# Paged decode of a hybrid layer step: all score products of a half batch in one run, six key buffers, and a first up pair of seven block products

## The chip, the cores and the metric

The kernel runs on one core of one Trainium2 chip. The metric is the device time of one launch in microseconds (us), the median of several runs; the time before is 1226.16 us. The core's engines work side by side, each through its own queue in order: TensorE (PE in the profile; PEld its weight loads), VectorE (DVE), ScalarE (ACT), GpSimd (POOL) and SyncE (SP, which issues most of the weight transfers).

## The reference

One layer of a hybrid decoder for 512 prompt tokens and 8 x 4 sample tokens, all in float32:

```python
def layer(h, pos, past_ckv, past_kr, ...):
    h = h + 0.5 * rmsnorm(swiglu(rmsnorm(h, norm_g[0]), wg[0], wu[0], wd[0]), norm_g[1])
    m, c_kv, k_r, s_fin = mixer(rmsnorm(h, norm_g[2]), ...)      # HGRN2 heads and latent attention heads
    h = h + rmsnorm(m, norm_g[3])
    h = h + 0.5 * rmsnorm(swiglu(rmsnorm(h, norm_g[4]), wg[1], wu[1], wd[1]), norm_g[5])
    return h, c_kv, k_r, s_fin
```

In the mixer each sample token attends to 4096 cached positions, whose latents (256 wide) and rotary keys (64 wide) lie in pages that a page table scatters over a pool. A score is the product of query and latent plus the product of the rotary parts; then softmax, then the weighted sum of the latents:

```python
s = (einsum('bqhr,bsr->bhqs', q_lat, c_kv) + einsum('bqhd,bsd->bhqs', q_rope, k_rope)) * scale
p = softmax(where(k_pos <= q_pos, s, -inf))
o = einsum('bhqs,bsr->bqhr', p, c_kv)
```

## The kernel before

The kernel keeps the layer's activations on the chip and streams the weights. Matrix products are made of three products of a high and a low half of each operand: `split` (lines 157 to 159) casts a tile to its high part on ScalarE and subtracts for the low part on VectorE, so every weight tile and every activation passes both engines (`wh` and `wl`, `uh` and `ul`, and so on).

**The decode.** The paged attention of the samples runs in small steps between the products of the mixer's big gemms (line 248), from about 705 to 920 us. Its 8 sample sequences are 16 half batches (class `Half`). A half gathers two blocks of latents (`gather`, into the slots `ma`, `dx0`, `dx1`, `q0`, `ha`, `hb`, `mb`) and their rotary keys (`rraw`) by indirect transfers. `turn` (line 1498) transposes them on VectorE into key tiles `kh`, one of five stages at a time, two transposes each; there are `KHB` = 4 buffers for `kh`. `score` (line 1510) makes eight small products for a stage, 64 rows by 32 columns of TensorE's array, so 40 for a half. When the last stage is done, ScalarE copies the odd half of the scores and VectorE adds and takes the maximum (`top`, line 1519). `peak` (from line 1523) spreads the maximum by a product `pm`, VectorE reduces it and makes the softmax's bias, ScalarE exponentiates, VectorE transposes the result (`pt`), and six copies on ScalarE and two on VectorE place it in `pbuf`. `value` (line 1546) then makes 16 products of `pbuf` and the latents.

The generator `decode` sets the order: for a half in step n come its `turn` in the steps after it, its scores two steps later, its peak and values three steps later. `RUNS` says in which of the five steps which stages are scored:

```python
RUNS = {2: (0, 1, 2), 4: (3, 4)}
```

so three stages (24 products) run in the middle step and two (16) in the last. Where these pieces come to stand between the gemm's products is decided ahead of the launch, by the scheduler that orders each engine's instructions; the early halves are cut into smaller pieces by it.

**The second FFN.** Gate and up weights come as pairs j = 4 to 10 of 128-column tiles (`tile_pair`). A pair takes one of two forms. `classic` (the products at line 230) makes four sums, each of 24 products of 128x272. `seven` (the products at line 449) makes seven block products of 12 each, in the banks X, Y and Z, from sums of the weight blocks (`S` and the in-place sums, lines 480 to 486) and of the activation blocks (`T1` to `T3` and the blocks `B11`, `B12`, `B21`, `B22`); ScalarE copies a bank to `tq` and VectorE adds up the results (line 498). Before, the first gate pair and the first up pair (j = `J0` = 4) are classic. Between the two, VectorE makes the activation sums for the later pairs, and the last of them, `split(*B12, Z)`, overwrites `B12`, which the classic up pair still reads; so it stands at the start of j = 5.

Of the kernel before, what the change touches and what calls it, by code (L numbers as in the profile page):

```python
# [15 lines left out]
ALU = mybir.AluOpType  # L16
# [43 lines left out]
NW = 2  # L60
PRE, BODY = 22, 95
JS = ((8, 9), (0, 1), (2, 3), (4, 5), (6, 7))
KHB = 4
PEAK = 1
RUNS = {2: (0, 1, 2), 4: (3, 4)}
LEVELS = (32, 16, 8, 4, 2, 1)
CH = 64

# [39 lines left out]
def hybrid_step_kernel(  # L108
# [18 lines left out]
    def mk(shape, dt, tag, bufs=1, pool=None):  # L127
        return (pool or cur[-1]).tile(shape, dt, name=tag, tag=tag, bufs=bufs)
# [28 lines left out]
    def split(hi, lo, src, eng=None):  # L157
        nc.scalar.copy(hi, src)  # L158
        (eng or nc.vector).tensor_tensor(lo, src, f32(hi), op=ALU.subtract)  # L159
# [160 lines left out]
    def raw_pair(src, f):  # L320
        return [raw(src, f + i) for i in range(2)]
# [15 lines left out]
    def wsplit(w, step=KD):  # L337
        ws = ring()
        for k in range(0, KD, step):
            split(*parts(ws, slice(k, k + step)), w[:, k : k + step])  # L340
        return ws
# [1078 lines left out]
    with scope("dec"):  # L1420
# [48 lines left out]
        class Half:  # L1469
# [31 lines left out]
            def score(self, st):  # L1501
                q = qbd[self.b % 2]
                if st == 0:
                    self.s = [ps("s", own=True) for _ in range(2)]
                for jj, j in enumerate(JS[st]):
                    for g in range(2):
                        c = (2 * jj + g) * 32
                        for r in range(2):
                            rs = slice(r * 64, r * 64 + 64)
                            nc.tensor.matmul(self.s[r][c : c + 32, : 2 * P], q[rs, j], self.kh[st][rs, g, :, jj], start=st == 0, stop=st == len(JS) - 1, skip_group_check=True)  # L1510
                if st == 1 and self.i and self.b + 1 < NB:
                    qsplit(self.b + 1)
                if st < len(JS) - 1:
                    return
                odd = mk([64, 2, 2 * P], F32, "odd")
                self.mx = mk([P, 1], F32, "mxh", 2)
                for r in range(2):
                    nc.scalar.copy(odd[:, r], self.s[r][64:, : 2 * P])
                    self.top = nc.vector.tensor_tensor_reduce(self.e[r * 64 : r * 64 + 64], self.s[r][:64, : 2 * P], odd[:, r], 1.0, -3.0e38, ALU.add, ALU.max, self.mx[r * 64 : r * 64 + 64])

            def peak(self):
                pm = ps("pm", "pm")[:, :P]
                nc.tensor.matmul(pm, self.mx.broadcast_to([P, P]), ident, start=True, stop=True, skip_group_check=True)
                m = m3[:, self.i, self.bs]
                nc.vector.tensor_reduce(m, pm.rearrange("p (g q) -> p q g", q=16), axis=AX.X, op=ALU.max)
                mq = mk([P, 16], F32, "mq", 2)
                mb = mk([P, 1], F32, "mbd", 2)
                nc.vector.scalar_tensor_tensor(mq, m, -SCALE, selL, op0=ALU.mult, op1=ALU.mult, accum_out=mb)
                nc.scalar.activation(self.e, self.e, AF.Exp, scale=SCALE, bias=mb, accum_out=Lc[:, self.i, 0, self.b : self.b + 1])
                pt = mk([P, ROWS, 32], F32, "pt", 2)  # L1530
                nc.vector.transpose(pt.rearrange("p a k -> p (a k)"), self.e)
                for r in range(2):
                    for g in range(2):
                        for h_ in range(2):
                            src = pt[(2 * r + g) * 32 : (2 * r + g) * 32 + 32, :, h_ * 16 : h_ * 16 + 16]
                            to = self.p[(2 * r + h_) * 32 : (2 * r + h_) * 32 + 32, g, :, self.i * 16 : self.i * 16 + 16]
                            (nc.scalar.copy if g + h_ else nc.vector.tensor_copy)(to, src)
# [19 lines left out]
        def decode():  # L1557
# [19 lines left out]
            for n in range(NH2 + 4):  # L1577
# [3 lines left out]

                for st in range(len(JS)):
                    if at(2):
                        for k in RUNS.get(st, ()):
                            at(2).score(k)
                    if n < 2 and st == 0:
                        if n == 0:
# [152 lines left out]
    with scope("ffn1") as pool:  # L1740
# [14 lines left out]
            nc.vector.tensor_tensor(mT[x][:, d], mT[x][:, d], acc, op=ALU.add)  # L1755

        def tile_pair(j, src, C, mid=None):
            if j == J0:
                w = ws.pop() if ws else [wsplit(w) for w in raw_pair(src, 2 * j)]
                classic(w, C, 0, ucol)  # L1760
                with tc.issue_after(mark[2]):
                    next(sc, None)
                classic(w, C, 1, ucol)
                if mid:
                    mid()
            else:
                seven(raw_pair(src, 2 * j), C, mid, sc if j < 7 else iter(()))

# [7 lines left out]
        for j in range(J0, NF // 2):  # L1776
            if j > J0:
                late = G, V
            G, V = (c[:, j % 2] for c in Cq)
            if j == J0 + 1:  # L1780
                with tc.issue_after(mark[0]):
                    split(*B12, Z)
            if j == 7:
                mT = [actslot("m", x, n=W2) for x in BOTH]
                for x in BOTH:
# [9 lines left out]
            if j == J0:  # L1795
# [9 lines left out]
                nc.vector.tensor_tensor(Z, f32(B21[0]), f32(B21[1]), op=ALU.add)  # L1805
                split(*T2, Y)
                nc.vector.tensor_tensor(Z, Z, Y, op=ALU.subtract)
            else:
                H = [mk([P, 2, 2, W2], F32R, n, 3) for n in ("hh", "hl")]
                with tc.issue_after(mark[0]):  # L1810
# [140 lines left out]
```

## Time and profile before

| | |
|---|---|
| median of the runs | 1226.16 us (1226.01 to 1227.58) |
| the profiled run, its own time | 1225.88 us |
| its span | 1224.0 us (1.88 us lie outside) |
| TensorE busy | 1197.8 us, 98% |
| weight loads busy | 1092.4 us, 89% |
| VectorE busy | 986.6 us, 81% |
| ScalarE busy | 693.6 us, 57% |
| GpSimd busy | 97.7 us, 8% |

The numbers come from one execution recorded by the hardware profiler. Busy time of an engine is summed over its instructions; a row of the timeline has the start, the duration, the engine, the line of the kernel, the operation with output and inputs, and, in brackets, for how long the engine had been idle and what released it. Rows that follow one another on an engine and are alike stand as one, with their count behind an x.

### The profile page before, as it was taken

The page shows a single profiled execution, that of the slowest core. Times are in us where ns is not written, and L with a number is a line of the kernel's source. Part 1 is how long each engine was busy: PE and PEld are TensorE (multiplying, and loading weights), DVE is VectorE, ACT ScalarE, POOL GpSimd, SP SyncE. Part 2 cuts the span into 40 slices and gives each one's busy share as a digit, 9 for nine tenths or more (in the row PEclk, how much of TensorE's full clock was granted, in tenths as well). Part 3 has the DMA queues.
Part 4 walks back from the last instruction along what each step waited for, and adds up shares of the span by engine and source line. Part 5 has one row for each costly group of instructions (what it writes and reads, how often), then busy time and mean ns, then how long its engine had stood idle before and what let it go on. Part 6 is the DMA issues. An engine that isn't in the chain of part 4 may idle for free.

```text
span 1224.0 us, 26742 instructions
## 1 busy us (share of the span) xinstructions
PE 1197.8 (98%) x10924; PEld 1092.4 (89%) x10924; DVE 986.6 (81%) x2008; ACT 693.6 (57%) x1447; POOL 97.7 (8%) x112
## 2 busy tenths in 40 slices
PE   8999999999999999999999999999999999999997
PEld 7999999999999989998998876666667999999996
DVE  7997887878678788886877789888985789778665
ACT  7765554454476654554758765455444465554373
POOL 0000000000000000000000123332321111000000
PEclk9999999999999999999999999999999999999999
DMA  6233333323254313333242486679876858533451
GB/s 242 70 121 104 104 101 94 101 80 105 83 186 142 116 56 104 90 92 108 95 141 86 163 343 209 231 266 356 277 258 163 262 211 286 163 107 118 103 149 74
DMA packets 78427, 188.43 MB, mean 154 GB/s; under 512 B 14032, under 2 KB 35568, under 8 KB 73824
## 3 DMA queue, kind: packets, MB, share of 16 engines
q1 hardware_dynamic: 58128, 115.50, 28.8%
q0 software_dynamic: 15440, 65.67, 16.5%
q10 hardware_dynamic: 4736, 5.55, 1.3%
q8 instruction: 85, 1.39, 0.5%
q14 instruction: 38, 0.31, 0.1%
HBM read 170.53 MB, written 16.16 MB: 153 GB/s over the span
## 4 chain that ended last, share of the span: by engine, by line
PE 81%; issue 6%; DVE 5%; ACT 3%; DMA 3%; POOL 1%; DVEq 0%; SPq 0%; ACTq 0%; POOLq 0%
PE acc L248 18%; PE dn L230 12%; PE Y L449 11%; PE acc L230 8%; PE Z L449 7%; PE X L449 7%; PE acc L1853 3%; PE acc L628 3%; PE s L1510 3%; PE o L1546 2%; DVE kh L1498 1%; DMA ma<-w_g 1%; PE pa L976 1%; DMA mb<-w_u 1%; PE s L1226 1%
## 5 line engine op out<-in xcount | busy, mean ns | idle before, releaser
L248 PE MATMUL acc<-uh,wh 128*128 128x272 f32 (+2 forms) x496 | 160.9, 324 | 0.0
L248 PE MATMUL acc<-ul,wh 128*128 128x272 f32 (+2 forms) x496 | 156.3, 315 | 1.0 <-DVE ul L196 1.0
L248 PE MATMUL acc<-uh,wl 128*128 128x272 f32 (+2 forms) x496 | 155.7, 314 | 0.5 <-issue 0.5
L230 PE MATMUL dn<-hh,dh 128*128 128x272 f32 x384 | 111.3, 290 | 0.1
L230 PE MATMUL dn<-hh,dl 128*128 128x272 f32 x384 | 110.7, 288 | 0.0
L230 PE MATMUL dn<-hl,dh 128*128 128x272 f32 x384 | 110.5, 288 | 0.0
L222 DVE TENSOR_TENSOR wl<-wraw,wh 128x1024 fp32r<-128x1024 f32 (+2 forms) x78 | 83.6, 1074 | 31.7 <-ACT wh L221 31.1
L248 PEld LDWEIGHTS acc<-uh,wh 128*128 128x128 f32 x496 | 93.4, 188 | 17.1 <-issue 12.7
L221 ACT CAST wh<-wraw 128x1024 fp32r<-128x1024 f32 (+2 forms) x78 | 72.6, 932 | 57.8 <-PE acc L248 37.8
L248 PEld LDWEIGHTS acc<-ul,wh 128*128 128x128 f32 x496 | 93.5, 188 | 7.7 <-DVE ul L196 2.0
L248 PEld LDWEIGHTS acc<-uh,wl 128*128 128x128 f32 x496 | 93.3, 188 | 6.3 <-issue 1.5
L230 PEld LDWEIGHTS dn<-hh,dh 128*128 128x128 f32 x384 | 72.3, 188 | 1.0 <-DVE ha L498 0.3
L230 PEld LDWEIGHTS dn<-hl,dh 128*128 128x128 f32 x384 | 72.4, 188 | 0.0
L230 PEld LDWEIGHTS dn<-hh,dl 128*128 128x128 f32 x384 | 72.2, 188 | 0.0
L158 ACT CAST wh<-wraw 128x512 fp32r<-128x512 f32 (+1 forms) x68 | 41.2, 643 | 46.8 <-PE Z L449 33.1
L158 ACT CAST sh<-wraw 128x512 fp32r<-128x512 f32 (+1 forms) x67 | 40.9, 651 | 32.0 <-PE Z L449 20.1
L158 ACT CAST dh<-wraw 128x512 fp32r<-128x512 f32 x48 | 29.7, 620 | 48.1 <-PE dn L230 46.1
L159 DVE TENSOR_TENSOR wl<-wraw,wh 128x512 fp32r<-128x512 f32 (+1 forms) x68 | 46.5, 717 | 5.1 <-ACT wh L158 3.8
L159 DVE TENSOR_TENSOR sl<-wraw,sh 128x512 fp32r<-128x512 f32 (+1 forms) x67 | 46.9, 724 | 1.5 <-ACT sh L158 0.8
L1510 PE MATMUL s<-kh,q 64*32 64x256 f32 x1280 | 47.2, 382 | 0.0
L1490 POOL DMA_INDIRECT rraw<-pool_r,idx x32 | 32.9, 1027 | 142.0 <-DVE kh L1498 105.2
L501 ACT COPY tq<-X 128x272 f32<-128x272 f32 x31 | 11.9, 385 | 54.9 <-PE X L449 54.3
(723 smaller groups left out, 4122.0 us busy)
## 6 DMA issues: line engine op xcount, KB each, us to landing
wraw<-w_u SPq DMA_DIRECT2D x44, 512.0 KB
wraw<-w_g SPq DMA_DIRECT2D x43, 512.0 KB
wraw<-w_d SPq DMA_DIRECT2D x24, 512.0 KB
wraw<-w_in SPq DMA_DIRECT2D x24, 512.0 KB
wraw<-w_o SPq DMA_DIRECT2D x16, 512.0 KB
wraw<-w_d SPq DMA_DIRECT2D x16, 384.0 KB
wraw<-w_d SPq DMA_DIRECT2D x16, 256.0 KB
mA<-s_post ACTq DMA_DIRECT2D x16, 136.0 KB
```

The costliest lines, as they stand in the source:

```text
L158: nc.scalar.copy(hi, src)
L159: (eng or nc.vector).tensor_tensor(lo, src, f32(hi), op=ALU.subtract)
L221: nc.scalar.copy(wh[:, :kt], w[:, :kt])
L222: low[0] = nc.vector.tensor_tensor(wl[:, :kt], w[:, :kt], f32(wh[:, :kt]), op=ALU.subtract)
L230: mark[2] = nc.tensor.matmul(out, a, b, start=n == 0, stop=n == last).ins
L248: nc.tensor.matmul(acc[:, :n], a[:, k], b[:, k], start=k + i == 0, stop=k == kt - 1 and i == 2)
L449: mark[2] = nc.tensor.matmul(bank, a[p][:, k], b[q][:, k], start=first and k + n == 0, stop=k == 3 and n == 2, skip_group_check=True).ins
L628: nc.tensor.matmul(accs[x, d], wts[d][p][:, k], hs[k // 2][q][:, k % 2, x], start=k + n == 0, stop=k == nf - 1 and n == 2)
L1490: nc.gpsimd.indirect_dma_start(rraw.rearrange("p a r -> p (a r)"), None, pool_r, off)
L1510: nc.tensor.matmul(self.s[r][c : c + 32, : 2 * P], q[rs, j], self.kh[st][rs, g, :, jj], start=st == 0, stop=st == len(JS) - 1, skip_group_ ...
L1546: nc.tensor.matmul(o[g : g + 32, :R], self.p[:, c, a], self.craw[c][:, a], start=i + c == 0 and a < 4, stop=i + c == 2 and a >= 4, skip_gr ...
L1853: nc.tensor.matmul(accs[x, d], wts[d][p][:, k], hs[k // 2][q][:, k % 2, x], start=k + n == 0, stop=k == nf - 1 and n == 2)
```

## The change

There are two parts.

In the decode all five stages of a half are scored in its last step (`RUN` = 4), `KHB` goes from 4 to 6, and the scratch tiles `odd` and `pt` become buffers of the shared scratch `ssq` and `sq1`, two of each, which other parts of the kernel use too.

In the second FFN the first up pair is made by `seven`, and `split(*B12, Z)` follows directly on the other activation sums.

```diff
-KHB = 4
+KHB = 6
-RUNS = {2: (0, 1, 2), 4: (3, 4)}
+RUN = 4
...
-                odd = mk([64, 2, 2 * P], F32, "odd")
                 self.mx = mk([P, 1], F32, "mxh", 2)
                 for r in range(2):
-                    nc.scalar.copy(odd[:, r], self.s[r][64:, : 2 * P])
-                    self.top = nc.vector.tensor_tensor_reduce(self.e[r * 64 : r * 64 + 64], self.s[r][:64, : 2 * P], odd[:, r], 1.0, -3.0e38, ALU.add, ALU.max, self.mx[r * 64 : r * 64 + 64])
+                    odd = tmp("ssq", 2 * P)[:64]
+                    nc.scalar.copy(odd, self.s[r][64:, : 2 * P])
+                    self.top = nc.vector.tensor_tensor_reduce(self.e[r * 64 : r * 64 + 64], self.s[r][:64, : 2 * P], odd, 1.0, -3.0e38, ALU.add, ALU.max, self.mx[r * 64 : r * 64 + 64])
...
-                pt = mk([P, ROWS, 32], F32, "pt", 2)
-                nc.vector.transpose(pt.rearrange("p a k -> p (a k)"), self.e)
+                pt = tmp("sq1", ROWS * 32)
+                nc.vector.transpose(pt, self.e)
+                pt = pt.rearrange("p (a k) -> p a k", k=32)
...
-                        for k in RUNS.get(st, ()):
+                        for k in range(len(JS)) if st == RUN else ():
                             at(2).score(k)
...
         def tile_pair(j, src, C, mid=None):
-            if j == J0:
-                w = ws.pop() if ws else [wsplit(w) for w in raw_pair(src, 2 * j)]
+            if j == J0 and ws:
+                w = ws.pop()
                 classic(w, C, 0, ucol)
                 with tc.issue_after(mark[2]):
                     next(sc, None)
                 classic(w, C, 1, ucol)
-                if mid:
-                    mid()
             else:
                 seven(raw_pair(src, 2 * j), C, mid, sc if j < 7 else iter(()))
...
-            if j == J0 + 1:
-                with tc.issue_after(mark[0]):
-                    split(*B12, Z)
...
                 nc.vector.tensor_tensor(Z, Z, Y, op=ALU.subtract)
+                with tc.issue_after(mark[0]):
+                    split(*B12, Z)
```

The list `ws` holds the weights of the first gate pair, which are loaded early; it is empty when the up pair comes.

The order of the instructions on each engine, before and after, differs in the stretches concerned and nowhere ahead of them. Three places follow.

On TensorE, around the half batch 3 (`s<-kh` are score products, `o<-ha` and `o<-hb` values, `pm` the spread maximum, `acc` the gemm), before:

```order
L1510 MATMUL s<-kh,q_8212 32x256 x24
L248 MATMUL acc<-uh,wh 128x512
L248 MATMUL acc<-ul,wh 128x512
L248 MATMUL acc<-uh,wl 128x512
L248 MATMUL acc<-uh,wh 128x512
L248 MATMUL acc<-ul,wh 128x512
L248 MATMUL acc<-uh,wl 128x512
L248 MATMUL acc<-uh,wh 128x512
L248 MATMUL acc<-ul,wh 128x512
L248 MATMUL acc<-uh,wl 128x512
L1510 MATMUL s<-kh,q_8212 32x256 x16
L1546 MATMUL o<-ha,pbuf 32x256 x8
```

and after, in the same place, with the end of the run of half 2 six gemm products ahead of the first row:

```order
L1523 MATMUL pm<-ident,mxh 128x128
L248 MATMUL acc<-uh,wl 128x512
L248 MATMUL acc<-uh,wh 128x512
L248 MATMUL acc<-ul,wh 128x512
L248 MATMUL acc<-uh,wl 128x512
L248 MATMUL acc<-uh,wh 128x512
L248 MATMUL acc<-ul,wh 128x512
L248 MATMUL acc<-uh,wl 128x512
L1510 MATMUL s<-kh,q_8212 32x256 x40
L1547 MATMUL o<-ha,pbuf 32x256 x8
L1547 MATMUL o<-hb,pbuf 32x256 x8
```

The 24 and the 16 products with nine gemm products between them have become one run of 40, and the runs of two halves stand thirteen gemm products apart here; in later halves 24 to 30. Over the whole decode there are 38 runs before and 28 after, for the same 640 products.

On VectorE, where the mixer's activations are split (`ul`) and the keys of the first halves are transposed (`kh`):

```order
 L794 TENSOR_TENSOR sil<-sil,acc 128x256
-L196 SCALAR_TENSOR_TENSOR ul<-mb,gv,uh 128x256
-L1498 STREAM_TRANSPOSE kh<-ma 128x512
-L1498 STREAM_TRANSPOSE kh<-dx_8785 128x512
-L196 SCALAR_TENSOR_TENSOR ul<-mb,gv,uh 128x256 x3
+L196 SCALAR_TENSOR_TENSOR ul<-mb,gv,uh 128x256 x4
 L283 TENSOR_TENSOR hh<-hh,s_post 128x512 x2
```

The two transposes between the first `ul` and the other three have moved ahead of this stretch.

On VectorE in the second FFN (`t3l`, `hh`: activation sums; `ul`: the low part of `B12`; `wl`, `sl`, `s4l`: low parts of weight blocks; line 498: results put together), before:

```order
L159 TENSOR_TENSOR t3l<-hl,t3h 128x1088
L1807 TENSOR_TENSOR hh<-hh,hl 128x1088
L482 TENSOR_TENSOR wraw<-wraw 128x512
L159 TENSOR_TENSOR sl<-wraw,sh 128x512 x2
L159 TENSOR_TENSOR sl<-S,sh 128x512
L486 TENSOR_TENSOR wraw<-wraw,S 128x512
```

and after:

```order
L159 TENSOR_TENSOR t3l<-hl,t3h 128x1088
L1803 TENSOR_TENSOR hh<-hh,hl 128x1088
L482 TENSOR_TENSOR wraw<-wraw 128x512
L486 TENSOR_TENSOR wraw<-wraw,S 128x512
L159 TENSOR_TENSOR wl<-S,wh 128x512
L159 TENSOR_TENSOR ul<-hh,uh 128x4x272
L159 TENSOR_TENSOR wl<-S,wh 128x512
L159 TENSOR_TENSOR sl<-wraw,sh 128x512 x2
L159 TENSOR_TENSOR s4l<-wraw,s4h 128x512
L498 TENSOR_TENSOR hb<-Y,tq 128x272
```

The split of `B12` has moved from behind eight further instructions to the middle of the up pair's weight splits, and the up pair's own block sums and splits have come in.

## Rows read from the trace of the kernel before

**Rows 1.** The page, part 1: busy time of each engine, its share of the span, instructions.
```profile
PE 1197.8 (98%) x10924; PEld 1092.4 (89%) x10924; DVE 986.6 (81%) x2008; ACT 693.6 (57%) x1447; POOL 97.7 (8%) x112
```

**Rows 2.** Windows of 100 us: length, busy time (instructions) by engine, granted clock, DMA.
```profile
800.00:900.00 100.00, 99.25 (x1168) 66.43 (x1167) 86.99 (x200) 48.81 (x122) 32.71 (x35) 1.00 0.86 299
900.00:1000.00 100.00, 99.01 (x1051) 82.65 (x1051) 72.96 (x134) 50.70 (x107) 16.41 (x21) 1.00 0.70 221
```

**Rows 3.** Timeline of TensorE: start, us, engine, line, operation, output and inputs, [idle before].
```profile
803.67 0.40 PE L248 MATMUL acc<-uh,wl 128*128 128x512 f32 x1
804.00 1.53 PE L1510 MATMUL s<-kh,q 64*32 64x256 f32 x48
805.46 0.50 PE L248 MATMUL acc<-uh,wh 128*128 128x512 f32 x1
805.79 0.39 PE L248 MATMUL acc<-ul,wh 128*128 128x512 f32 x1
806.02 0.39 PE L248 MATMUL acc<-uh,wl 128*128 128x512 f32 x1
...
808.43 1.09 PE L1510 MATMUL s<-kh,q 64*32 64x256 f32 x32
809.46 1.07 PE L1546 MATMUL o<-q,pbuf 128*32 128x256 f32 x16
```

**Rows 4.** Timeline of the weight loads around the first of these runs.
```profile
804.00 1.04 PEld L1510 LDWEIGHTS s<-kh,q 64*32 64x32 f32 x48 [0.37 <-issue]
805.45 0.19 PEld L248 LDWEIGHTS acc<-uh,wh 128*128 128x128 f32 x1 [0.41 <-issue]
```

**Rows 5.** Timeline of TensorE in the first half batch.
```profile
726.22 0.39 PE L248 MATMUL acc<-ul,wh 128*128 128x256 f32 x1 [0.96 <-DVE ul L196]
...
730.63 0.28 PE L248 MATMUL acc<-uh,wh 128*128 128x256 f32 x1
730.84 0.62 PE L1510 MATMUL s<-kh,q 64*32 64x256 f32 x4
...
731.61 0.29 PE L248 MATMUL acc<-uh,wl 128*128 128x256 f32 x1
```

**Rows 6.** Timeline of VectorE in front of that wait.
```profile
725.13 0.66 DVE L1498 STREAM_TRANSPOSE kh<-dx 128x512 f32<-128x512 f32 x1
725.72 1.23 DVE L196 SCALAR_TENSOR_TENSOR ul<-mb,gv,uh 128x256 fp32r<-128x256 f32 x3
```

**Rows 7.** Timeline of TensorE in a late half: peak product and values.
```profile
898.68 0.38 PE L1523 MATMUL pm<-ident,mxh 128*128 128x128 f32 x2
...
905.37 0.85 PE L1546 MATMUL o<-hb,pbuf 128*32 128x256 f32 x12 [0.85 <-ACT pbuf L1537]
```

**Rows 8.** Timeline of VectorE in the same stretch.
```profile
900.45 0.25 DVE L1525 TENSOR_REDUCE q<-pm 128x16 f32<-128x128 f32 x1
900.62 1.21 DVE L222 TENSOR_TENSOR wl<-wraw,wh 128x1024 fp32r<-128x1024 f32 x1
...
906.36 0.42 DVE L1519 CUSTOM_DVE_ANT_0 q<-s,odd 64x256 f32<-64x256 f32 x1 [0.63 <-ACT odd L1518]
```

**Rows 9.** Timeline of ScalarE in the same stretch.
```profile
904.10 1.84 ACT L1537 COPY pbuf<-pt 32x128 f32<-32x128 f32 x6 [0.94 <-DVE pt L1531]
```

**Rows 10.** Timeline of TensorE: the first score run of an early half.
```profile
769.14 2.09 PE L1510 MATMUL s<-kh,q 64*32 64x256 f32 x48
```

**Rows 11.** Line 1498, the key transposes: count, ns min/median/max, first and last start.
```profile
L1498 DVE STREAM_TRANSPOSE kh<-dx x40: 662/670/714, 709.2 to 914.0; 128x512 f32<-128x512 f32 x40
```

**Rows 12.** Timeline of ScalarE: copies of two sums in the first up pair.
```profile
975.75 0.39 ACT L353 COPY hb<-acc 128x272 f32<-128x272 f32 x1 [1.23 <-PE acc L230]
978.78 0.39 ACT L353 COPY hb<-acc 128x272 f32<-128x272 f32 x1 [2.64 <-PE acc L230]
```

**Rows 13.** Timeline of VectorE in the second FFN.
```profile
988.28 1.29 DVE L159 TENSOR_TENSOR ul<-hh,uh 128x1088 fp32r<-128x1088 f32 x1 [4.79 <-ACT uh L158]
...
995.75 0.43 DVE L498 TENSOR_TENSOR ha<-Y,tq 128x272 f32<-128x272 f32 x1
```

## The prediction, made before the changed kernel was run

> **What bounds the kernel now.** I read the engine totals first: TensorE's matmul row is busy 98% of the span, the next engine, VectorE, 81% [rows 1]. The 100 us windows then show that this holds in the two stages that the change touches: TensorE 99% with VectorE at 87% while the paged decode runs (800 to 900 us), TensorE 99% with VectorE at 73% where the second FFN begins (900 to 1000 us), and a granted clock of 1.00, the upper level of 2.4 GHz, in both [rows 2]. So what counts is what TensorE executes and the small stretches in which it waits. Three views price that: the timeline of TensorE around the score runs, the timeline of the engines that feed it, and the rows of the transposes that make the keys.
>
> **The decode, what is taken away.** The program has 16 half batches of 40 score products each, 640 products, which the profile shows as 1280 records (two for a product, so the order's x24 is its x48). A gemm step takes 0.23 us (805.79 to 806.02 in [rows 3]). Beside such steps a run of 48 records costs this: from the last gemm step before it at 803.67 to the second one behind it at 806.02 are 2.35 us, in which three steps of 0.23 lie, so 1.66 us are the run's. A run of 32 begins 1.03 us before its successor, one of 48 begins 1.46 before [rows 3]: 0.43 us for 16 records, 0.027 each. Then 48 records are 1.29 us and 0.37 us are fixed per run. Very short runs have a floor: 4 records lie between 730.63 and 731.61, 0.98 us with two gemm steps of 0.12 in it, so 0.74 us [rows 5].
>
> In the order TensorE has 38 score runs before and 28 after (16 would be one per half; the scheduler still splits six halves). Before, 6 have at most 5 products (28 records together), 32 are longer (1252 records): 6 x 0.74 + 32 x 0.37 + 1252 x 0.027 = 50.1 us. After, 7 short ones (18 records) and 21 longer (1262): 7 x 0.74 + 21 x 0.37 + 1262 x 0.027 = 47.0 us. That is -3.1 us. One value run, of the half 1, now stands alone in the gemm instead of right behind a score run, which costs one more fixed part, +0.4. **Fewer runs: -2.7 us.** All of it is on TensorE's path.
>
> The Trainium skill, "TensorEngine Tiling (Array Packing)", section Key Properties, says that changing the tiling mode drains TensorE. The weight loads show gaps of that kind on both sides of a run, 0.37 us into it and 0.41 us out of it [rows 4]. If each such pair were lost whole, ten runs fewer would be 10 x 0.78 = 7.8 us by that rule; what the runs of 32 and 48 take apart says 0.37, because part of the gap lies under matmuls still in flight, and I go by 0.37.
>
> **Two waits that go.** At 726.22 us TensorE waits 0.96 us for a `ul` that VectorE made at 725.72, after a key transpose at 725.13 and another before it [rows 5, 6]. In the new order these two transposes stand earlier, and the four `ul` follow one another, so the wait goes: -1.0 us. At 905.37 us a value run waits 0.85 us for ScalarE's copies into `pbuf` [rows 7]. Their chain is the peak product at 898.68, a reduce that starts behind transposes at 900.45, then a weight split of 1.21 us on VectorE before the softmax scale can follow [rows 7, 8], then the copies at 904.10 [rows 9]. The new order has no weight split between reduce and scale there: -0.85 us. **Together -1.8 us.**
>
> **Waits that come.** With all five stages in one run, all keys of a half must be there before the run ends, and six buffers hold only one stage of the next half ahead. VectorE makes the other four, 8 transposes 0.6 us apart (0.67 each, overlapping a little [rows 11]) and three short instructions, 5.4 us, after the two maxima of the half before; these take about 1.4 us from the end of a run (0.63 for the copy of the odd half, then twice 0.42 [rows 8]). So the keys are complete some 6.8 us behind the end of a run. In an ordinary half TensorE first has 16 value products (about 1 us, by the 1.07 of a row of them [rows 3]), 24 gemm steps (5.5 us), the peak and the switch (0.5 us), and reaches the last stage 1.7 us into the run: about 8.8 us. VectorE has up to 1.9 us of gemm work between, so it just holds. Halves 2 and 3 are the exception: only 6 + 7 gemm steps stand between their runs, and TensorE wants the last stage after 0.4 + 13 x 0.23 + 0.5 + 1.7 = 5.6 us. It waits 1.2 us by this sum; up to 3.5 us if ScalarE's 1.84 us of copies [rows 9] and one gemm instruction of VectorE come ahead, none if the maxima are quicker. I take 1.5 us, near the sum. Against it goes a wait of today inside the run at 769.14, which takes 2.09 us instead of 1.53 [rows 3, 10]: -0.55 us. **Net +0.95 us**, bounds -0.55 to +2.95.
>
> The value run's `pbuf` is a second one: four halves now have only 12 gemm steps and the run (2.8 + 2.5 = 5.3 us) between peak and values; the chain of [rows 7 to 9] is 6.7 us with the 1.13 us of weight split in it, 5.5 without. **+0.6 us**, bounds 0 to +1.5. The load of a sample residue into the shared scratch moves behind a few weight loads on the SyncE queue; that queue has nothing due for ten microseconds then, so I cost it at nothing, covered by TensorE's gemm; were the cover gone, the weight load behind it would be late by that transfer.
>
> **The second FFN's first up pair.** Four sums of 24 products become seven of 12: 96 to 84. The copies of two sums' results lie 3.03 us apart [rows 12], 24 steps, so 0.126 us each: -1.5 us. The block form has hand-offs which the plain one lacks: a bank copied before it is summed into again (0.39 us on ScalarE [rows 12], about 0.25 of it seen), a bank drained and combined on VectorE (0.43 us [rows 13] plus a drain, 0.7 us where two products on Y follow each other), and the first split of pair 5 (0.3 us). VectorE gets some 6.4 us more to do; it idles 4.79 us at 983.5 to 988.28 [rows 13], the rest fits under TensorE because the window is 73% [rows 2]. **Net -0.25 us.** The bounds are -1.5 (all hand-offs hidden) and +1.3: the split of the last block operand, today at 988.28 [rows 13], must move to about 980, behind the sums for the T operands and a few shorter instructions, and TensorE wants it at about the same time.
>
> **Sum.** -2.7 - 1.8 + 0.95 + 0.6 - 0.25 = -3.2 us on the profiled run of 1225.88 us: 1222.7. The median of the runs is 0.28 us above it (1226.16): **1223.0 us**. With every bound low: -4.5 - 0.55 - 1.5 = -6.55, so 1219.6; with every bound high: -4.5 + 2.95 + 1.5 + 1.3 = +1.25, so 1227.4.
>
> **Rivals.** First, *new waits take the place of the old ones*: halves 2 and 3 cost their upper end (+2.95), the FFN its upper end (+1.3), the values +0.6: -4.5 + 4.85 = +0.35 us, 1226.5. For it: VectorE is at 87% in the decode, and every key now has an earlier deadline. Against it: its gemm work between the transposes has not grown.
>
> Second, *slower, through the keys of every half*: the margin of an ordinary half is 0.1 to 2 us (8.8 against 6.8 and up to 1.9 of other work). If VectorE is later than that, each of the 13 or so remaining halves waits. The wait at 769.14 is the nearest price, 0.56 us [rows 3, 10]: 13 x 0.56 = 7.3 us, and the sum becomes +4.1, 1230.3 us. It decides as soon as the average half loses more than 3.2/13 = 0.25 us. For it speaks that VectorE's work sits between the transposes in an order fixed beforehand, so one late `acc` holds all transposes behind it; VectorE's in-order queue did just that at 726.22 [rows 5, 6]. Against: today's halves need three stages at a time and four buffers, and wait only at 769.14 and in small amounts elsewhere.
>
> Third, *each run removed is worth its two gaps* (by the rule above, 7.8 us in place of 3.1): -3.2 - 4.7 = -7.9, 1218.3 us. The traces speak against it with 0.37 [rows 3].
>
> That the change does not do what it says is half true already: 28 runs and not 16 are in the sum.
>
> **How the numbers follow.** Forecast 0.47 (its own range 1220.5 to 1225.0), first rival 0.28, second 0.17, third 0.08. A measurement of this kernel tells about 0.2%, 2.45 us, from no change: faster means under 1223.7, slower over 1228.6. Faster: the third rival and nine tenths of the forecast, 0.08 + 0.42 = 0.50. Slower: the second rival, 0.17. Same: 0.33. The range reaches from the low sum, 1219.5, to 1228.5, beyond the high sum, where it takes in a second rival that is only half as dear; it leaves out the third rival and most of the second, some 0.2.
>
> **What the profile after would show.** 28 score runs, the long ones of 80 records lasting about 2.2 us and followed at once by values; no wait for `ul` near 726 and none of 0.85 at the late value run; one wait in the run of half 3, under 2 us. The up pair shorter by one to two microseconds between its gate pair and pair 5. Wrong would be: score runs of 80 records that last clearly over 2.3 us in most halves (second rival), or an up pair as long as before with TensorE waiting for the late split (first).

## The result: 0.8% slower, and the profile after

The changed kernel takes 1236.54 us (median of 6 runs, 1234.82 to 1240.44), the kernel before 1227.15 us beside it (6 runs); the ratio is 1.0081, with a 95% interval of 1.0070 to 1.0093. I had forecast 1223.0 us, 0.3% faster. The profiled run took 1234.93 us, its span is 1233.2 us, 9.2 us longer than before.

Part 1 of the page of the changed kernel, columns as in [rows 1], and then two of its windows, columns as in [rows 2]:

```profile
PE 1200.3 (97%) x10912; PEld 1095.5 (89%) x10912; DVE 991.6 (80%) x2022; ACT 696.0 (56%) x1450; POOL 98.6 (8%) x112
```

```profile
800.00:900.00 100.00, 96.53 (x1104) 64.59 (x1104) 83.25 (x196) 49.42 (x124) 31.22 (x32) 1.00 0.82 285
900.00:1000.00 100.00, 98.97 (x1070) 80.10 (x1073) 75.37 (x143) 50.53 (x106) 18.65 (x23) 1.00 0.70 216
```

TensorE has its 12 products less (x10912 for x10924), but in the decode it is busy 96.5% of the window where it was 99.3%, and VectorE is busy less too, 83% for 87%: neither got fuller, both wait more. To see where, I set equal gemm products (line 248) of the two traces side by side. The changed kernel is 0.65 us behind at 722 us, ahead of the first score products, and 8.25 us behind at 924 us and after; points between tell little, because a product can stand before a score run in one order and behind it in the other. In the second FFN the changed kernel gets back to 6.7 behind by 1020 us and is 9.3 behind at 1065. So in this pair of traces the decode lost 7.6 us, 1.6 came back, and something after that lost 2.7.

Of the 1.6 us only 0.2 are the up pair's. The other 1.4 are a wait for a transfer at 1005 us in the trace of the kernel before. The decode's part alone (below), which has the old FFN but not this wait, gains the same 1.4 us there:

```profile
1005.49 0.30 PE L1328 MATMUL sr<-mb,sq 128*32 128x128 f32 x2 [0.96 <-DMA mb<-w_u]
```

Nor are the 7.6 us the change's alone: in both traces single runs of small products hold time that belongs to no instruction (last section).

The waits of TensorE from 715 to 945 us, first of the kernel before, then of the changed one (us in total, times, longest):

```profile
PE o L1546 <- ACT pbuf L1537: 1.3, 2, 0.8
PE acc L248 <- DVE ul L196: 1.0, 1, 1.0
...
PE b L1451 <- DVE mxh L1519: 0.4, 1, 0.4
```

```profile
PE acc L248 <- DVE wl L222: 4.4, 4, 1.8
PE b L1451 <- DVE mxh L1519: 1.9, 1, 1.9
PE o L1547 <- ACT pbuf L1538: 0.7, 2, 0.4
```

The wait for `ul` is gone, as foretold; in its place stand four waits for `wl`, the low part of a gemm weight, which the kernel before does not have here and for which the prediction has no price, and a longer one for the maxima of the samples' own attention (`b`). The rest sits inside score runs, where the matmul rows hide it and the weight loads show it (waits of the weight loads, before and after):

```profile
PEld s L1510 <- issue: 5.5, 15, 0.4
PEld s L1510 <- DVE kh L1498: 2.2, 7, 0.4
```

```profile
PEld s L1510 <- issue: 9.5, 22, 0.6
...
PEld s L1510 <- DVE kh L1498: 1.9, 4, 0.8
```

Counting only the gaps of over 0.1 us between weight loads of one run, so without the entry into a run: 1.0 us before, 7.7 us after.

**A wait for wl, read closely.** ScalarE, VectorE and TensorE of the changed kernel, on the weight that TensorE waits for at 785 us:

```profile
769.02 1.05 ACT L221 CAST wh<-wraw 128x1024 fp32r<-128x1024 f32 x1 [0.81 <-PE acc L248]
```

```profile
777.43 1.90 DVE L1498 STREAM_TRANSPOSE kh<-dx 128x512 f32<-128x512 f32 x3
...
783.69 0.43 DVE L1531 STREAM_TRANSPOSE sq<-q 128x256 f32<-128x256 f32 x1
784.04 1.19 DVE L222 TENSOR_TENSOR wl<-wraw,wh 128x1024 fp32r<-128x1024 f32 x1
```

```profile
785.29 0.50 PE L248 MATMUL acc<-uh,wl 128*128 128x512 f32 x1 [1.81 <-DVE wl L222]
```

and the same weight in the kernel before:

```profile
771.91 1.05 ACT L221 CAST wh<-wraw 128x1024 fp32r<-128x1024 f32 x1 [1.49 <-PE acc L248]
```

```profile
773.42 1.20 DVE L222 TENSOR_TENSOR wl<-wraw,wh 128x1024 fp32r<-128x1024 f32 x1
```

```profile
782.93 0.39 PE L248 MATMUL acc<-uh,wl 128*128 128x512 f32 x1
```

The raw weight and its high part are there in good time in both, the high part even 3 us earlier in the changed kernel. In the kernel before VectorE makes the low part at once, at 773.42, 8 us ahead of its use. In the changed kernel `wl` stands in VectorE's order behind the keys of two halves (16 transposes after the cast), the maxima and the softmax, and is made at 784.04. TensorE does not come early: it would take this product at 783.5 us, where it took it at 782.93 before. The delay is VectorE's alone.

### The profile page after: what moved, and what is told of

Read it like the earlier page. It is cut to its first block, busy times and chain, and to the rows that moved or that the text cites. A ratio compares the mean times of both kernels' runs of the same rounds, so it can differ in the third digit from the quotient of the medians.

```text
span 1233.2 us, 26716 instructions
## 1 busy us (share of the span) xinstructions
PE 1200.3 (97%) x10912; PEld 1095.5 (89%) x10912; DVE 991.6 (80%) x2022; ACT 696.0 (56%) x1450; POOL 98.6 (8%) x112
## 4 chain that ended last, share of the span: by engine, by line
PE 82%; DVE 9%; ACT 4%; DMA 3%; issue 2%; SPq 0%; DVEq 0%; ACTq 0%
PE acc L248 20%; PE dn L230 11%; PE Y L449 10%; PE acc L230 9%; PE Z L449 7%; PE X L449 7%; PE acc L628 3%; PE s L1510 3%; DVE kh L1498 2%; PE acc L1851 2%; PE o L1547 2%; DMA wraw<-w_u 1%; DMA wraw<-w_g 1%; PE pa L976 1%; PE sr L1328 1%
## 5 line engine op out<-in xcount | busy, mean ns | idle before, releaser
L158 ACT CAST sh<-wraw 128x512 fp32r<-128x512 f32 (+1 forms) x69 | 42.1, 650 | 37.0 <-PE Z L449 22.9
L1510 PE MATMUL s<-kh,q 64*32 64x256 f32 x1280 | 52.0, 381 | 1.4 <-issue 0.3
L1510 PEld LDWEIGHTS s<-kh,q 64*32 64x32 f32 x1280 | 26.0, 106 | 22.1 <-issue 9.5
```

## The experiments

The chips of the experiments run the kernel before in 1221 to 1223 us; each ratio is to runs of it on the same chip. The first three take the change apart.

**The decode's part alone** is the changed kernel without the two hunks of the diff in the FFN.

> The decode's part of the change alone (one score run per half, six key buffers, shared scratch); the second FFN as in the kernel before. Theory, from the two traces: the decode loses all of it. In the trace of the changed kernel the gemm of the mixer is 0.65 us behind the kernel before at 722 us and 8.25 us behind at 932 us, so this kernel should be slower by about 7.6 us, 1233 to 1235 us, with score runs that stall inside for 7 to 8 us in all (1.0 before) and waits for weight splits of 4 to 5 us. Rival: the two parts hurt each other, and the loss comes mostly from the FFN and from scheduling around it; then this kernel is within 3 us of the kernel before.

1.0045 (1.0029 to 1.0061): the decode's part loses 5.5 us by itself, less than the 7.6 that I expected. The waits for weight splits are there (5.7 us); the stalls inside score runs are 2.5 us and not 7 to 8.

**The up pair alone** is the kernel before with these two hunks; it was run twice, the second time on the chip of the kernel with the loads behind.

> The second FFN's part alone: the first up pair as seven block products and the earlier split of B12; the decode as in the kernel before. Theory: it is worth its twelve products, since the changed kernel makes up 1.6 us between 960 and 1020 us; 1224 to 1225.5 us. Rival: the later waits in the changed kernel (0.86 us at 1057 and 1.35 us at 1063 us, on sums of VectorE, where it falls back by 2.7 us) belong to this part; then the gain is eaten, and the kernel is at 1226.5 to 1228 us.

1.0015 (1.0002 to 1.0028). The rival holds: the part does not win but loses, and its trace has the later waits. The 1.6 us that the theory counts on were mostly the transfer wait at 1005 us.

> The second FFN's part alone once more, as the base for the kernel with the loads behind, on the same chip and in more rounds: +0.1 to +0.2% against the kernel before, with the two waits for sums on Y (0.9 and 1.8 us) again and the loads of mA again ahead of the weight tile. If the order of the two transfers is chance, the loads come behind it in this execution, and the waits are gone.

1.0015 (1.0004 to 1.0025), the same waits and the same order of transfers.

**Buffers alone**: the decode's part with the old runs.

```diff
-RUN = 4
+RUNS = {2: (0, 1, 2), 4: (3, 4)}
```

> Six key buffers and the shared scratch as in the changed kernel, but the scores in two runs per half (three stages, then two) as in the kernel before; the FFN as before. If the single run is what costs, this kernel is at or a little under the kernel before: waits for keys inside score runs go (about 2 us listed for key transposes before), 1224 to 1226.5 us. If the order that goes with six buffers (transposes ahead of weight splits on VectorE) or the shared scratch is what costs, it is slower by 3 us or more, with waits for weight splits as in the changed kernel.

0.9998 (0.9985 to 1.0012). Six buffers and the shared scratch are not the loss. They do bring three of the four waits for `wl` (3.3 us, at the same three gemm products as in the decode's part alone) and the 1.9 us at `b`. They pay for them inside the score runs: the scheduler leaves 32 runs here, two for each half and none cut, where the kernel before has 38, and TensorE is busy 42.5 us with score products where that order takes 47.0. The single run in the last step is what turns level into 5.5 us: score products take 46.7 us again, although there are only 28 runs, because the first half is in eight pieces, five later halves in two, and half 3 waits for its keys; and the wait at 785 us comes on top. Why the scheduler cuts halves in one order and not in the other stays open.

**The run one step earlier**: the decode's part with

```diff
-RUN = 4
+RUN = 3
```

> The decode's part alone, with the single score run one step earlier (RUN = 3 in place of 4); FFN as before. In the order there are 21 score runs instead of 28. Theory: the run in the last step costs because its 24 earlier products used to stand ahead of weight splits and gave them time; TensorE then comes early to the gemm and waits for wl. A run one step earlier gives part of that time back and leaves one step more between the maxima and the values: waits for wl fall from 5.7 to under 3 us, and the kernel is 2 to 6 us faster than the decode part with RUN = 4, 1221 to 1226 us where that one is at 1228. Rival: the keys are the limit; with the run earlier they are later still, waits inside the runs grow to over 5 us, and the kernel is slower than with RUN = 4.

0.9993 (0.9983 to 1.0002), 0.5% better than RUN = 4, by that one number. TensorE's waits from 715 to 945 us, RUN = 4 (the decode's part alone) and then RUN = 3:

```profile
PE acc L248 <- DVE wl L222: 5.7, 4, 1.9
PE b L1451 <- DVE mxh L1519: 1.9, 1, 1.9
```

```profile
PE acc L248 <- DVE wl L222: 2.5, 3, 1.4
PE tp L1455 <- DVE q L1556: 1.4, 1, 1.4
```

The waits for `wl` are more than halved, as expected, and the one at 785 us is gone: VectorE makes that weight's `wl` at 770.00. So a run of five stages is no loss as such; its place is. The theory's picture, that the 24 earlier products gave the splits time, is not what the rows at 785 us show: TensorE came no earlier there, the split came later.

**Two runs, the first one step later** asks whether the place of the first 24 products alone decides:

```diff
-RUN = 4
+RUNS = {3: (0, 1, 2), 4: (3, 4)}
```

> The decode's part alone with two score runs per half and six buffers, but the first run (24 products) one step later than in the kernel before, in step 3 in place of 2. 35 score runs in the order. It tells the place of the first 24 products from the number of runs. Theory: what the single run in the last step loses is that these 24 products no longer stand ahead of the weight splits; moved by one step of two, half of that is lost, waits for wl of 4 to 5 us (3.3 with both runs in their old steps, 5.7 with all in the last), and the kernel is 0.2 to 0.4% slower than the kernel before. Rival: the number of products in one run is what costs (all five stages' keys at once); then two runs cost nothing wherever they stand, and the kernel is within 0.1% of the kernel before.

0.9993 (0.9982 to 1.0005), with 2.4 us of waits for `wl`. My expectation failed: a step later costs nothing, there is no slope from step 2 to step 4. Together with RUN = 3 this says that the loss belongs to the combination, all 40 products in the last step, and not to late first products in general. The traces of these orders, side by side (TensorE, us; the stretch lies between the two gemm products that the kernel before makes at 722 and 932 us; busy from part 5 of the pages; waits are those listed from 715 to 945 us):

| | stretch | busy with score products | waits |
|---|---|---|---|
| order of the kernel before (the three traces with the new FFN alone) | 204.8 | 47.0 | 2.7 |
| buffers alone | 205.5 | 42.5 | 7.2 |
| two runs, the first a step later | 205.2 | 44.1 | 5.2 |
| RUN = 3 | 205.0 | 42.1 | 5.8 |
| RUN = 4, the decode's part alone | 210.9 | 46.7 | 9.1 |
| first measurement, kernel before | 210.0 | 47.2 | 3.9 |
| first measurement, changed kernel | 217.6 | 52.0 | 8.1 |

Each order with six buffers waits more than the old one. Three get that back in cheaper score runs; all 40 products in the last step do not, and wait longest.

**Keys once**: two kernels leave out four of five key transposes, so that VectorE is relieved of them, in one run and in two per half.

```diff
             def turn(self, st):
+                if st:
+                    return
...
-... self.kh[st][rs, g, :, jj] ...
+... self.kh[0][rs, g, :, jj] ...
```

> The decode's part alone, with 4 of 5 key transposes left out: stages 1 to 4 of a half score against the keys of stage 0, so these scores are not those of the reference. 16 halves, 20 score runs in the order. With VectorE relieved of 128 transposes (77 us) what is left is TensorE's own price of a run. Theory: no wait for keys or weight splits is left in the decode (under 1 us), and against the same kernel in two runs (the next one, 33 runs in the order) it gains 13 x 0.37 = 4.8 us. Rival, the whole gap at both ends of a run: 13 x 0.78 = 10 us. Rival, a run of 80 records is limited by TensorE's own issue, so that stalls of 0.5 us stay inside the runs without any work for VectorE: gain under 2 us.

> The same omission (keys of stage 0 for all stages) with six buffers and the scores in two runs per half as in the kernel before: 33 score runs in the order. It is the base for the kernel above. Theory: faster than the kernel before by what VectorE's keys cost there, the listed waits inside runs and for ul, pbuf and peak, 2 to 5 us; slower than the single run by 4.8 us. Rival: the keys cost nothing in the kernel before, and this one is within 1 us of it.

1.0045 (1.0031 to 1.0060) and 1.0061 (1.0044 to 1.0078): both slower than the kernel before, with 128 transposes less. Inconclusive for the price of a run: without the transposes the scheduler lays out another order, and TensorE meets other waits (`b` for the maxima 5.2 us in the kernel with two runs, a weight split 4.3 us in the one with one), with lowered clock behind them. My expectation that under 1 us of waits would be left failed. They show two things. Most runs of 80 records in the first take 2.32 us with no gap over 0.1 us inside, so such a run is not held up by TensorE itself; the exceptions are a run at the lowered clock, 3.54 us, and one of 2.88 us at 769 us. And VectorE's load alone does not set the time: it is busy 122 us of 230 in the one-run kernel, and 195 us in the decode's part, which has the same ratio.

**The changed kernel again:**

> The changed kernel once more, beside the next three on one chip. By the two parts measured apart (+0.45% and +0.15%) it should be 0.5 to 0.7% slower than the kernel before. Theory: its trace shows the waits for weight splits of the decode part (4 to 6 us) and the waits of the second FFN at about 1057 and 1063 us again, while the 5 us of stalls inside four score runs that no instruction explains (three or four products per 0.75 us) come and go from one execution to another. Rival: those stalls belong to the changed kernel; then they are there again, at the same runs, and the kernel is 0.8% slower or more.

1.0075 (1.0058 to 1.0092), a little over the 0.5 to 0.7% of the parts added. Waits for `wl` 6.0 us, `b` 1.9, the waits of the FFN as before; the gaps inside runs are 3.1 us instead of 7.7, and 0.6 of them lie at a lowered clock. The theory holds for these gaps, with one open end (below).

**The loads behind the weight.** In the FFN part alone VectorE and TensorE look like this behind 1020 us:

```profile
1039.35 0.69 DVE L480 TENSOR_TENSOR S<-wraw 128x512 f32<-128x512 f32 x1 [5.99 <-DMA wraw<-w_u]
```

```profile
1045.91 0.39 PE L449 MATMUL Y<-t4h,wh 128*128 128x272 f32 x1 [0.89 <-DVE ha L498]
...
1052.47 0.39 PE L449 MATMUL Y<-uh,wh 128*128 128x272 f32 x1 [1.79 <-DVE ha L498]
```

VectorE idles 6 us for a raw weight tile of up pair 7, then runs behind its sums until TensorE waits twice. The queues of that kernel, SyncE's and GpSimd's (SPq rows take two issues together: the second of the `w_u` goes out at 1030.3):

```profile
1020.91 9.76 SPq L317 DMA_DIRECT2D wraw<-w_u  x2
...
1028.73 0.91 POOL L1782 DMA_DIRECT2D ma<-mA  x1 [11.21 <-PE sr L1328]
1029.63 0.89 POOL L1782 DMA_DIRECT2D mb<-mA  x1
```

and of the kernel before:

```profile
1025.55 4.70 SPq L317 DMA_DIRECT2D wraw<-w_u  x2
...
1033.35 0.91 POOL L1787 DMA_DIRECT2D ma<-mA  x1 [11.17 <-PE sr L1328]
1034.26 0.89 POOL L1787 DMA_DIRECT2D mb<-mA  x1
```

GpSimd's two loads (2 MB) are released by TensorE's sample products `sr`; they stand 4.6 us earlier here, as TensorE does (most of that lead is time which the trace of the kernel before lost in the gaps inside its value runs and at 1005 us). The weight tile is released by VectorE's splits, which have 6.4 us more to do by the prediction's count and did not get earlier. So they changed places, and not by chance: in all seven traces with the old FFN the tile goes out 3.3 to 3.4 us ahead of the loads, in all five with the new one and unheld loads 1.6 to 1.8 us behind them. The experiment moves the loads behind `late_w` and lets them wait for the tile (the loop around these lines is cut):

```diff
+                    nc.gpsimd.tensor_copy(mT[x][:, 0, :1], late_w[1][:, 0, :1])
                     nc.gpsimd.dma_start(mT[x][:, :, :n], mA[0][:, :, even[x].start : even[x].start + n])
```

(`late_w` is the raw pair of up pair 7, taken ahead of `seven`.)

> The second FFN's part alone, with one thing more: the two loads of mA for the sum mT (2 MB, on GpSimd's queue) wait until the second weight tile of up pair 7 has landed (a copy of one column of it into mT stands ahead of them). In the trace of the FFN part alone these loads go out at 1028.7 and 1029.6 us, ahead of that weight tile at 1030.3; it lands 9.0 us later, VectorE idles 5.99 us for it, and TensorE then waits 0.89 and 1.79 us for sums on Y. In the kernel before the weight tile goes out first (1029.9, the loads at 1033.4 and 1034.3) and lands 4.5 us later. Theory: the loads in front are the cause; with them behind, the 2.7 us of waits go and the part is worth its 1.6 us or more: 0.1 to 0.3% faster than the kernel before, 2 to 3 us faster than the part alone. Rival: VectorE is behind by its 6.4 us of extra work whatever the transfers do; then the waits stay, on the same sums, and the time is that of the part alone, +0.1 to +0.2%.

0.9995 (0.9986 to 1.0004), against 1.0015 of the part alone on the same chip: 2.4 us back. Against the kernel before, the 0.1 to 0.3% that I expected are not shown: the gain is 0.6 us, with an interval across zero, and the prediction's -0.25 us fits it. VectorE's wait at the same sum, and GpSimd's loads:

```profile
1033.77 0.69 DVE L480 TENSOR_TENSOR S<-wraw 128x512 f32<-128x512 f32 x1 [0.42 <-DMA wraw<-w_u]
...
1034.95 0.91 POOL L1821 DMA_DIRECT2D ma<-mA  x1 [0.32 <-POOL mb L1820]
```

The tile, issued at 1030.34 as in the part alone, is used 3.4 us later instead of 9.0; both waits on Y are gone. The transfer order is the cause of these 2.4 us, and it is shown.

**Both parts mended.**

> The changed kernel with RUN = 3 alone as its mend. If the two parts are independent, -0.07% and +0.15% add up to +0.05 to +0.15%, and against the changed kernel (+0.75%) it gains 7 to 9 us by one number. If the single run of five stages is a loss in whatever step, it stays over +0.4%.

1.0003 (0.9991 to 1.0015): by the one number RUN = 3 the changed kernel's +0.75% are gone.

> The changed kernel with the score run one step earlier (RUN = 3) and the two loads of mA behind the weight tile, as in the kernel above. If the three mends add up: -0.9 us of the decode with RUN = 3, -1.6 to -2.5 us of the FFN: 0.2 to 0.3% faster than the kernel before. If the FFN's loss comes back through another transfer or through VectorE, it is level with the kernel before.

0.9987 (0.9978 to 0.9996): with the loads behind as well, 1.6 us faster than the kernel before, the only one of these kernels whose interval lies under 1. It is less than the 0.2 to 0.3% that I had expected, and on the side forecast.

## Why the prediction was wrong, step by step

- **TensorE as the bound, VectorE beside it.** Right as a share of time, wrong as a guide. I took a VectorE at 87% and 73% as cover. What counted was when single instructions of its queue come, not how full it is: in the changed kernel it is emptier and TensorE waits more.
- **Price of a run, -2.7 us.** The price is right where it can be read. In undisturbed late halves of the decode's part, two halves (peak to peak) take 22.18 us with two runs, and 22.88 us with four in the FFN part alone, whose decode is the old one: 0.35 us for a run, where I had 0.37. Rows of the one, then of the other:

```profile
867.84 0.38 PE L1523 MATMUL pm<-ident,mxh 128*128 128x128 f32 x2
...
890.02 0.38 PE L1523 MATMUL pm<-ident,mxh 128*128 128x128 f32 x2
```

```profile
873.52 0.38 PE L1523 MATMUL pm<-ident,mxh 128*128 128x128 f32 x2
...
896.40 0.39 PE L1523 MATMUL pm<-ident,mxh 128*128 128x128 f32 x2
```

  So the third rival (0.78 us a run, the drain at both ends) falls: of the gaps that the weight loads show at both ends about half is paid. But the saving did not come over the whole decode. The terms of the runs, -2.7 and +0.95, make -1.75 us; measured, all but the listed waits changed by 6.1 - 6.4 = -0.3 us (in the table above, RUN = 4 against the order of the kernel before: 210.9 for 204.8, waits 9.1 for 2.7). RUN = 3 lets six gemm steps stand between run and values, pays the fixed part for the values again, and has little left of the saving (23.22 us for two halves, 0.57 of them a wait for `pbuf`).
- **Two waits that go, -1.8 us.** The one for `ul` went. The one for `pbuf` at 905 us is gone too, but it was not the order's: the same order in the FFN part alone had 0.5 us of such waits in the decode, where the profiled run of before had 1.3. I had counted one execution's chance as the program's.
- **Keys of half 3, +1.5 us, and -0.55 us against it.** The first is right in place and nearly in size. The second did not come: the run of half 2, which holds that wait today, still takes 2.88 us where undisturbed runs of 80 records take 2.32. The weight loads of that run wait 0.22 + 0.52 + 0.42 + 0.78 = 1.94 us for key transposes:

```profile
770.96 1.04 PEld L1510 LDWEIGHTS s<-kh,q 64*32 64x32 f32 x48 [0.37 <-issue]
772.22 0.17 PEld L1510 LDWEIGHTS s<-kh,q 64*32 64x32 f32 x4 [0.22 <-DVE kh L1498]
772.91 0.17 PEld L1510 LDWEIGHTS s<-kh,q 64*32 64x32 f32 x12 [0.52 <-DVE kh L1498]
773.51 0.14 PEld L1510 LDWEIGHTS s<-kh,q 64*32 64x32 f32 x4 [0.42 <-DVE kh L1498]
774.43 0.17 PEld L1510 LDWEIGHTS s<-kh,q 64*32 64x32 f32 x12 [0.78 <-DVE kh L1498]
```

- **pbuf, +0.6 us.** 0.7 us listed, in two places; the order of before has 0.5 at the first of them, so 0.2 are new.
- **What the sum left out, the step that failed.** "VectorE has up to 1.9 us of gemm work between, so it just holds" asks only whether the keys are in time for the run. I never asked the reverse: whether the gemm's work, now behind the keys in VectorE's order, is in time for the gemm. I named what stands between the transposes and priced only the transposes; the weight splits stood in the sum at nothing. For the waits outside the runs I had -1.8 + 0.6 = -1.2 us. Measured, the decode's part alone against the order of before, they are +6.4 us (2.7 to 9.1): `wl` 5.2 more, `b` 1.5 more. That is the decode's loss, with next to nothing gained in the runs to set against it. The order showed it: in the later halves `wl` stands behind the peak's chain, and I noted that only as a gain for that chain. Of the four waits for `wl` only the one at 785 us, 1.8 us, belongs to the single run; the other three and the one at `b` come with six buffers and are there in two runs too.
- **The second rival** had the sign and the engine, and with +4.1 us a size near the 5.5 us of the decode's part, but not the mechanism: it made every half wait for its keys. The keys were late in half 3 only; four times in the decode the late thing was a weight split.
- **The gaps inside runs.** In the first trace of the changed kernel four late runs contain 5 us that belong to no instruction. In the second trace of the same kernel and in that of the decode's part alone they are not there. They are not the program's, and the loss is there without them (0.75%). The prediction itself was drawn from a trace that has such gaps in its value runs.
- **The up pair, -0.25 us.** Right for the pair itself: against the last product of the mixer's gemm, the products of pair 5 stand 0.2 us earlier than with the old pair in each of the traces, and the hand-off on Y, for which I had 0.7 us, is 0.6 (a wait at 990.5 us). What failed is behind it: what I put down as hidden, the rest of VectorE's 6.4 us, is what made it late with releasing the tile buffers, so that the load of `mA`, which follows TensorE, came first. I had asked which products wait for VectorE, not which transfers do.

## What to carry to other kernels

When a run of small work is moved on a saturated engine, ask of each engine that feeds it not only whether the moved work gets its inputs in time, but also which other work now stands behind those inputs and when that is due: here the low part of a weight stood behind sixteen transposes that had become urgent. Count an order by its deadlines, engine by engine, and not by busy shares. And where two queues are released by different engines, an edit that moves one of these engines by a few microseconds can exchange two transfers; see which of them is urgent before counting the gain.

## What the runs showed of the hardware

A wait on TensorE can cost more than its length. In the second trace of the changed kernel the product behind the 1.93 us wait at 752.35 and the gemm products after it run at the lower of the two levels (1.2 GHz of 2.4) until 755.5; the mean granted clock of the stretch from 752 to 756 us is 0.57. Gemm steps take 0.43 us there (753.80 to 754.22) and 0.23 afterwards. Windows (columns as in [rows 2]) and timeline of that kernel:

```profile
748.00:752.00 4.00, 2.37 (x33) 1.31 (x33) 4.00 (x6) 2.77 (x7) 2.59 (x3) 1.00 0.26 69
752.00:756.00 4.00, 3.65 (x11) 3.13 (x12) 3.94 (x11) 0.96 (x3) 1.84 (x2) 0.57 0.92 318
756.00:760.00 4.00, 4.00 (x20) 3.29 (x19) 2.83 (x9) 0.61 (x3) 0.00 (x0) 1.00 1.02 410
```

```profile
752.35 1.22 PE L1451 MATMUL b<-ident,rs_t 128*128 128x128 f32 x4 [1.93 <-DVE mxh L1519]
...
753.80 0.63 PE L248 MATMUL acc<-uh,wl 128*128 128x512 f32 x1
754.22 0.63 PE L248 MATMUL acc<-uh,wh 128*128 128x512 f32 x1
...
756.10 0.39 PE L248 MATMUL acc<-uh,wl 128*128 128x512 f32 x1
```

From 752.35 to 755.5 at half the clock is about 1.6 us lost beside the wait itself. The same wait in the decode's part alone (1.93 us) and in the first trace (1.95 us) was not followed by it, so it comes in some executions only. The kept traces tell more of it. Ahead of the decode, where all orders are alike and TensorE waits 0.5 us at 694 and 0.6 to 0.9 us at 698, the lower level comes in 12 of the 14 traces, for about 3 to 8 us; in the kernel before and in one other it does not. The changed kernel is 1.7 us behind the kernel before at 700 us and still 0.65 at 722. The same four microseconds before and after the change:

```profile
698.00:702.00 4.00, 4.00 (x32) 3.86 (x33) 3.06 (x5) 4.00 (x7) 1.97 (x2) 1.00 0.99 332
```

```profile
698.00:702.00 4.00, 3.86 (x19) 3.86 (x20) 3.06 (x6) 3.12 (x6) 2.14 (x2) 0.57 1.01 329
```

Open stays what makes the gaps inside single runs of small products. In the first trace of the changed kernel, weight loads of one run:

```profile
887.87 0.17 PEld L1510 LDWEIGHTS s<-kh,q 64*32 64x32 f32 x3 [0.37 <-issue]
888.62 0.16 PEld L1510 LDWEIGHTS s<-kh,q 64*32 64x32 f32 x4 [0.58 <-issue]
889.38 0.62 PEld L1510 LDWEIGHTS s<-kh,q 64*32 64x32 f32 x22 [0.60 <-issue]
```

Three or four loads pass per 0.75 us, where 22 pass in 0.62 right after. They occur in four of the 28 score runs of that execution, all beside an indirect gather on GpSimd; other runs beside such a gather have none. The kernel before has the same in the first measurement, in its value runs:

```profile
822.19 0.16 PEld L1546 LDWEIGHTS o<-mb,pbuf 128*32 128x32 f32 x5 [0.58 <-issue]
822.91 0.17 PEld L1546 LDWEIGHTS o<-mb,pbuf 128*32 128x32 f32 x3 [0.56 <-issue]
```

TensorE is busy 33.9 us with values in that trace and 32.4 in that of the changed kernel, against 30.9 in every trace of the experiments. So these gaps are in both traces of the first measurement and in none of the twelve others. In the first measurement the kernel before also took about 1227 us, and on the chips of the others 1221 to 1223; whether the two belong together was not measured.
